# State-space hand-over by halves of the last down slice, low halves of y ahead of the second scan, later scans in parts

## The chip, the cores and the metric

The kernel runs on one core of one Trainium2 chip. The metric is the device time of one execution in microseconds (us). The core has a matrix engine (TensorE, PE in the profile; PEld is its weight load), a vector engine (VectorE, DVE), an activation engine (ScalarE, ACT), a general engine (GpSimd, POOL) and a queue of DMA issues (SyncE, SP). Each engine runs its own instructions in the order in which the program was laid out for it, and waits for others by semaphores.

## The reference

A trunk of two layers over 256 tokens with 2048 features, all in float32. Layer 0 mixes tokens with a convolution module, layer 1 with a state-space module; each is followed by a dense MLP.

```
x = x + conv_module(rms_norm(x))         # layer 0
x = x + mlp(rms_norm(x))                 # relu(h @ w_up)^2 @ w_down, 2048 -> 8192 -> 2048
# layer 1: h = rms_norm(x), 128 groups of 16 features, 64 complex states each
s_t = a * s_{t-1} + B u_t                # scan over the 256 tokens
y   = gelu(C s + d * h)
x   = x + val * sigmoid(gate)            # val, gate = split(y @ w_glu), 2048 -> 4096
x = x + mlp(rms_norm(x));  out = rms_norm(x)
```

## The kernel before

**Weights.** All dense weights stream through the core once. A *step* is one 1 MB tile of weights (`raw`), loaded by an SP DMA into one of three slots, and it has two *halves*. `split` (L109) makes of each half a rounded high part (`hi`, a copy on ACT, L117) and a remainder (`lo`, a subtraction on DVE, L119), each into one of four slots, and TensorE multiplies three times, hi by hi, lo by hi and hi by lo. `run_steps` (L148) walks the halves: before it consumes half h it issues splits up to half h + 3, so that the split of half h + 4 can start when half h has been consumed and its slot is free. Splits have a high priority in the list that the planner sorts by. The planner lays out each engine's order by a simulated timeline; `behind(ins)` (L391) makes the instructions of a block follow `ins` on its own engine.

**The last down slice of layer 0.** `mlp.down` (L697) multiplies by w_down in slices of 512 output columns. The last slice is consumed by `consume_by_block` (L712): it holds the weights of all its four halves, finishes token block 0 first, then the first 256 columns of block 1, then the other 256. After each piece `last_add` (L748) adds it to x and sums squares (on ACT for the first two pieces, on DVE for the last), and `block_rstd` (L760) makes the norm factor of a block; `ssm_block` (L166) turns the factors into the small matrix `rs` and starts the last `ssm_slice` (L1107), which writes a slice of x to DRAM and reads it back as `xJ`, tokens in chunks of eight.

**The state-space module.** Its input is cut into four parts B = 0 to 3 of 512 features. For one part: `chunks` (L1132) reorders xJ and turns it on PE (`ut`), `ssm_scale` multiplies by the norm factors, `ssm_front` (L1203) multiplies by the table W and copies to X, `ssm_turn` (L1219) turns X into PSUM (`xtr`), `ssm_scan` (L1230) does on DVE six products and sums, two scans, two products that turn back, and four sums into `SS`; `ssm_local` (L1263) multiplies by M, `ssm_carry` (L1278) by V onto the same banks, and takes the GELU on ACT into `y`; `ssm_out` (L1294) turns y (`yt`) and splits it into hi and lo as `yT`, with `hsplit` (L224).

**The GLU.** `glu` (L1308) has 16 steps, numbered (i, half). `begin` (L1321) stands between the last down step and the first GLU step and runs parts 0 and 1 of the state-space work: the first four GLU halves are split there (`more`, L1315), two before the first scan, one behind it, one behind the second. `keep_warm` (L173) puts multiplications by the identity on PE between the pieces. The first GLU product needs both halves hi and lo of yT of part 0. The rest of the state-space work is hung onto GLU steps by the dictionary `todo` (L1383): part 1 is multiplied at steps 1 and 2, parts 2 and 3 follow in pieces from step 1 to step 12. In it `chunk3` (L1358) turns part 3's input at step (3, 1), and `ssm_scan(2)` and `ssm_scan(3)` stand at (3, 0) and (6, 1), each as a whole.

Of the kernel before, what the change touches and what calls it, by code (L numbers as in the profile page):

```python
# [18 lines left out]
P = 128  # L19
# [17 lines left out]
class Trunk:  # L37
# [71 lines left out]
    def split(self, h, urgent=True):  # L109
        i, half = divmod(h, 2)  # L110
        raw = self.raws[i] if half == 0 else self.raws.pop(i)
        nk = raw.shape[1] // 2
        sl = raw[:, half * nk:(half + 1) * nk]
        hi = self.w.tile([P, nk] + list(raw.shape[2:]), F32R, tag="hi", name="hi", bufs=4)
        lo = self.w.tile([P, nk] + list(raw.shape[2:]), F32R, tag="lo", name="lo", bufs=4)
        with self.tc.high_priority(offset=URGENT if urgent else 0):
            self.nc.scalar.activation(hi, sl, AF.Copy)  # L117
            eng = self.nc.gpsimd if i in self.pool_lo else self.nc.vector
            ins = eng.tensor_tensor(out=lo, in0=sl, in1=hi.bitcast(F32), op=ALU.subtract)  # L119
            if i in self.pool_lo:  # L120
                self.pool_ins = ins
        self.parts[h] = (hi, lo)

# [24 lines left out]
    def run_steps(self):  # L148
        n = 2 * len(self.steps)
        ns = 0  # L150
        for h in range(n):
            i, half = divmod(h, 2)
            _, _, consume, pre = self.steps[i]
            if i == self.barrier and half == 0:
                self.barrier = None
                self.presplit = h
                pre()
                pre, ns = None, self.presplit
            while self.loaded < min(len(self.steps), i + 4):
# [12 lines left out]

    def keep_warm(self, n, after):  # L173

        ps = self.bank([P, P], name="warm")
# [496 lines left out]
    def mlp(self, layer, last_slice, last_block, hooks=None):  # L672
# [24 lines left out]
        def down(s):  # L697
            for n in range(NS):
                by_block = s == nsl - 1 and n == NS - 1
                for kc in range(2):  # L700
# [38 lines left out]
                    self.add_t(w_dn, s * 8 + kc * 4, n * 512, consume_by_block if by_block else consume,  # L739
# [367 lines left out]
    def ssm_slice(self, n):  # L1107
# [36 lines left out]
        def transposes(xr):  # L1144
            for g in range(0, 8, 4):
                ps = self.bank([P, 4, P], name="ut")
                for gg in range(4):
                    nc.tensor.transpose(ps[:, gg, :], xr[:, g + gg].rearrange("p t c -> p (t c)"), self.ident)
# [28 lines left out]
    def ssm_start(self):  # L1177
# [3 lines left out]
        with self.behind(self.mm_last):  # L1181
            self.late[0]()
        self.keep_warm(6, self.mm_last)
        nc.tensor.matmul(ps, lhsT=self.rowsel.rearrange("p t c -> p (t c)"),
                                   rhs=rs.rearrange("p b j -> p (b j)"), start=True, stop=True)
# [44 lines left out]
    def ssm_scan(self, B):  # L1230

        nc = self.nc
        ps, R = self.X.pop(B), self.tables.pop(("R", B))
# [16 lines left out]
        for i in range(2):  # L1250
            nc.vector.tensor_tensor_scan(out=flat(S[:, i]), data0=flat(m), data1=flat(S[:, i]), initial=0.0,
                                         op0=ALU.mult, op1=ALU.add)
        b = lambda i: R[:, i].unsqueeze(1).broadcast_to([P, 2, 16, 32])
        self.tt(t[:, 0], b(0), S, ALU.mult)
        self.tt(t[:, 1], b(1), S, ALU.mult)
# [22 lines left out]
    def ssm_carry(self, B):  # L1278
# [5 lines left out]
        if B == 0:  # L1284
            self.keep_warm(16, self.mmm)
        for g in range(8):
# [21 lines left out]
    def glu(self):  # L1308
# [6 lines left out]
        def more(n, xev=None):  # L1315
            for _ in range(n):
                with self.behind(self.scaled), self.behind(xev or self.scaled):
                    self.split(self.presplit, False)
                self.presplit += 1

        def begin():  # L1321
# [5 lines left out]
            more(2)  # L1327
# [23 lines left out]
            more(1, xev)  # L1351
# [5 lines left out]

        def chunk3():  # L1358
            late = []
            self.chunks[3](late)  # L1360
            with self.behind(self.mm_last):
                late[0]()
            self.ssm_scale(3)
# [15 lines left out]

        def front(B):  # L1380
            with self.behind(self.mm_last):
                self.ssm_front(B)
        todo = {(1, 0): (lambda: local(1), lambda: self.ssm_scale(2)), (1, 1): (lambda: carry(1),),  # L1383
                (2, 0): (lambda: out(1), lambda: front(2)), (2, 1): (lambda: turn(2),),
                (3, 0): (lambda: self.ssm_scan(2),), (3, 1): (chunk3,), (5, 0): (lambda: local(2),),
                (6, 0): (lambda: front(3),), (6, 1): (lambda: turn(3), lambda: self.ssm_scan(3)),
# [125 lines left out]
```

## Time and profile before

| | |
|---|---|
| device time, median of 3 runs (lowest to highest) | 2012.29 us (2011.23 to 2012.68) |
| the profiled execution: device time, span in the trace | 2011.6 us, 2009.8 us |
| PE busy, share of the span | 1977.3 us, 98% |
| PEld, DVE, ACT, POOL busy | 1693.9, 1399.2, 950.4, 280.6 us |
| mean granted TensorE clock | 0.996 |
| DMA | 428.49 MB, mean 213 GB/s |

Times in the rows below are counted from the first instruction of the span; the difference between device time and span, 1.8 us, lies around it. The last down slice of layer 0 runs from 1046 to 1057 us, `begin` from there to about 1088, the GLU steps to about 1294, and the MLP of layer 1 after that.

### The profile page before, as it was taken

How to read it: one execution, taken by the hardware profiler on the slowest of the kernel's cores; microseconds unless marked ns; L12 is line 12 of the kernel's file. 1: busy time of each engine (PE TensorE's matmuls, PEld its weight loads, DVE VectorE, ACT ScalarE, POOL GpSimd, SP SyncE). 2: the span in 40 equal slices, each digit the busy share in tenths (PEclk: the TensorE clock that was granted, in tenths of full speed). 3: DMA queues.
4: the chain of work that ended last, by engine and by line, in shares of the span. 5: the costliest groups of instructions: out<-in, count | busy, mean ns of one | idle time of the engine just before them, and what ended most of it. 6: DMA issues, size and time to landing. Idle time of an engine off the chain costs nothing.

```text
span 2009.8 us, 28976 instructions
## 1 busy us (share of the span) xinstructions
PE 1977.3 (98%) x11640; PEld 1693.9 (84%) x11640; DVE 1399.2 (70%) x1905; ACT 950.4 (47%) x1172; POOL 280.6 (14%) x257
## 2 busy tenths in 40 slices
PE   8999999999999999999998999999999999999998
PEld 8999787888888888888886788888888888888887
DVE  7899899967776777776557747565556555565655
ACT  6444654444444544444443445554444444444444
POOL 3998301000000221222010000000000000000000
PEclk9999999999999999999999999999999999999999
DMA  8668458766866877877887865665656666575653
GB/s 233 190 173 217 141 199 262 229 228 191 262 189 188 220 235 245 263 249 241 321 287 269 285 210 184 194 181 186 199 187 191 188 189 195 184 223 185 198 189 126
DMA packets 317030, 428.49 MB, mean 213 GB/s; under 512 B 9761, under 2 KB 211553, under 8 KB 313537
## 3 DMA queue, kind: packets, MB, share of 16 engines
q1 hardware_dynamic: 301120, 384.85, 60.9%
q0 software_dynamic: 12352, 37.49, 6.2%
q10 hardware_dynamic: 3424, 4.30, 0.8%
q8 instruction: 91, 1.49, 0.3%
q14 instruction: 43, 0.35, 0.0%
HBM read 400.08 MB, written 34.91 MB: 216 GB/s over the span
## 4 chain that ended last, share of the span: by engine, by line
PE 92%; DVE 5%; DMA 1%; issue 1%; POOL 0%; ACT 0%; ACTq 0%; SPq 0%; POOLq 0%; DVEq 0%
PE acc L187 23%; PE acc L210 15%; PE acc L212 15%; PE acc L211 15%; PE acc L190 12%; PE acc L199 3%; PE acc L201 3%; PE acc L200 3%; DVE lo L119 1%; DVE S L791 1%; PE pk L472 1%; DMA raw<-in_conv_w_in_dram 1%; DVE ws L791 1%; PE kp L1084 0%; DMA raw<-in_mlp_w_up_dram 0%
## 5 line engine op out<-in xcount | busy, mean ns | idle before, releaser
L117 ACT ACTIVATE hi<-raw 128x1024 fp32r<-128x1024 f32 x672 | 711.8, 1060 | 968.0 <-PE acc L212 524.8
L119 DVE TENSOR_TENSOR lo<-raw,hi 128x1024 fp32r<-128x1024 f32 x612 | 747.6, 1223 | 522.2 <-ACT hi L117 513.2
L187 PE MATMUL acc<-hT,hi 128*128 128x512 f32 x2048 | 516.1, 394 | 3.0 <-DVE t L779 2.1
L187 PEld LDWEIGHTS acc<-hT,hi 128*128 128x128 f32 x2048 | 369.7, 189 | 72.2 <-DVE t L779 2.4
L210 PE MATMUL acc<-hi,rT 128*128 128x512 f32 x992 | 387.4, 391 | 0.0
L211 PE MATMUL acc<-lo,rT 128*128 128x512 f32 x992 | 386.3, 389 | 0.0
L212 PE MATMUL acc<-hi,rT 128*128 128x512 f32 x992 | 385.9, 389 | 0.0
L190 PEld LDWEIGHTS acc<-hT,lo 128*128 128x128 f32 x2048 | 279.5, 190 | 20.9 <-DVE lo L119 0.8
L190 PE MATMUL acc<-hT,lo 128*128 128x256 f32 x2048 | 286.1, 282 | 0.4 <-DVE lo L119 0.4
L210 PEld LDWEIGHTS acc<-hi,rT 128*128 128x128 f32 x992 | 186.2, 188 | 39.9 <-issue 1.8
L212 PEld LDWEIGHTS acc<-hi,rT 128*128 128x128 f32 x992 | 186.2, 188 | 39.1
L211 PEld LDWEIGHTS acc<-lo,rT 128*128 128x128 f32 x992 | 186.3, 188 | 37.8
L119 POOL TENSOR_TENSOR lo<-raw,hi 128x1024 fp32r<-128x1024 f32 x60 | 143.3, 2406 | 31.3 <-ACT hi L117 31.2
L199 PE MATMUL acc<-hT,hi 128*128 128x256 f32 x512 | 146.2, 286 | 1.1 <-ACT hi L117 1.0
L200 PE MATMUL acc<-hT,hi 128*128 128x256 f32 x512 | 145.7, 286 | 0.0
L201 PE MATMUL acc<-hT,lo 128*128 128x256 f32 x512 | 145.5, 286 | 0.0
L800 DVE SCALAR_TENSOR_TENSOR cv<-vT,dw,cv 128x256 f32<-128x256 f32 x348 | 141.2, 482 | 2.2 <-ACT cv L515 1.7
L791 DVE TENSOR_TENSOR x<-x,acc 128x1024 f32<-128x1024 f32 (+1 forms) x72 | 83.6, 1161 | 33.5 <-PE acc L212 22.8
L212 PE MATMUL acc<-hi,yT 128*128 128x512 f32 x256 | 101.7, 397 | 4.8 <-DVE yT L226 4.8
L210 PE MATMUL acc<-hi,yT 128*128 128x512 f32 x256 | 102.6, 401 | 1.3 <-ACT hi L117 1.3
L211 PE MATMUL acc<-lo,yT 128*128 128x512 f32 x256 | 101.2, 395 | 1.6 <-DVE lo L119 1.6
L199 PEld LDWEIGHTS acc<-hT,hi 128*128 128x128 f32 x512 | 98.9, 193 | 3.4 <-ACT hi L117 1.7
(274 smaller groups left out, 1732.7 us busy)
## 6 DMA issues: line engine op xcount, KB each, us to landing
raw<-in_mlp_w_up_dram SPq DMA_DIRECT2D x128, 1024.0 KB, 5.8
raw<-in_mlp_w_down_dram SPq DMA_DIRECT2D x128, 1024.0 KB, 5.2
raw<-in_ssm_w_glu_dram SPq DMA_DIRECT2D x32, 1024.0 KB, 5.5
raw<-in_conv_w_in_dram SPq DMA_DIRECT2D x60, 512.0 KB, 5.6
raw<-in_conv_w_out_dram SPq DMA_DIRECT2D x16, 1024.0 KB, 5.2
Vd<-bv POOLq DMA_DIRECT2D x16, 512.0 KB, 4.9
Md<-Kd POOLq DMA_DIRECT2D x32, 256.0 KB, 7.9
Wt<-Wd SPq DMA_DIRECT2D x8, 1024.0 KB, 8.6
```

Source lines behind the costliest of these rows:

```text
L117: self.nc.scalar.activation(hi, sl, AF.Copy)
L119: ins = eng.tensor_tensor(out=lo, in0=sl, in1=hi.bitcast(F32), op=ALU.subtract)
L187: mm(accs[m], lhsT=hi[:, kk, cs[m]], rhs=xT(k0 + kk), start=first and kk == 0, stop=False)
L190: mm(accs[m][:, 0:T], lhsT=lo[:, kk, cs[m]], rhs=xT(k0 + kk)[:, 0, :], start=False, stop=last and kk == 3)
L199: mm(accs[m], lhsT=hi[:, kk, c], rhs=x[:, 0, :], start=first and kk == 0, stop=False)
L200: mm(accs[m], lhsT=hi[:, kk, c], rhs=x[:, 1, :], start=False, stop=False)
L201: mm(accs[m], lhsT=lo[:, kk, c], rhs=x[:, 0, :], start=False, stop=last and kk == 3)
L210: mm(acc[:, b, :], lhsT=ak[:, 0, t], rhs=hi[:, kk, :], start=first and kk == 0, stop=False)
L211: mm(acc[:, b, :], lhsT=ak[:, 0, t], rhs=lo[:, kk, :], start=False, stop=False)
L212: self.mm_last = mm(acc[:, b, :], lhsT=ak[:, 1, t], rhs=hi[:, kk, :], start=False, stop=last and kk == 1)
L791: self.nc.vector.tensor_tensor(out=out, in0=a, in1=b, op=op)
L800: return self.nc.vector.scalar_tensor_tensor(out=out, in0=a, scalar=s, in1=b, op0=op0, op1=op1)
```

## The change

Four things change. (1) In layer 0 the last down slice is consumed half by half (`consume_by_half`): each half is multiplied into all three pieces at once, and in the last half each piece is added to x as it is finished. Up to three GLU halves may then be split ahead of `begin` by the ordinary walk. (2) In `begin` the two splits ahead of the first scan and the one behind it are gone, one split remains behind the scans of part 1; part 3's reordering and turn (`chunks[3]`) come from step (3, 1) into `begin`, behind part 2's; the warming multiplications are 8 instead of 16 ahead of the first carry, and they follow part 3's turn; the carry takes the groups of the first SS half before those of the second. (3) `ssm_scan` is cut into three functions, and the scans of part 1 are put behind the low half of part 0's yT. (4) For parts 2 and 3 the scans, the products behind them and the sums into SS stand at steps of their own, each behind the newest low half of the weights (`lo_ins`).

```diff
@@ split, run_steps
             if i in self.pool_lo:
                 self.pool_ins = ins
+            else:
+                self.lo_ins = ins
...
-                self.presplit = h
+                self.presplit = ns
...
-            while ns < min(n, h + 4, n if self.barrier is None else 2 * self.barrier):
+            while ns < min(n, h + 4, n if self.barrier is None else 2 * self.barrier + 3):
@@ hsplit
-        self.nc.vector.tensor_tensor(out=lo, in0=raw, in1=hi.bitcast(F32), op=ALU.subtract)
+        self.low = self.nc.vector.tensor_tensor(out=lo, in0=raw, in1=hi.bitcast(F32), op=ALU.subtract)
@@ mlp.down
+                    def consume_by_half(hi, lo, half, kc=kc):
+                        if kc == 0 and half == 0:
+                            rT["acc"] = self.acc2()[:, 0, :], *(self.bank([P, 256], name="acc") for _ in range(2))
+                        h = kc * 2 + half
+                        for i, (b, c) in enumerate(((0, slice(0, 512)), (1, slice(0, 256)), (1, slice(256, 512)))):
+                            with self.behind(self.mm_last):
+                                self.mm_b(rT["acc"][i], lambda kk: rT[s][:, 2 * h + kk], hi, lo, b, c, h == 0, h == 3)
+                            if h == 3:
+                                self.last_add(b, int(i == 2), c, rT["acc"][i])
+                                if i:
+                                    last_block(i - 1)
...
+                               consume if not by_block else consume_by_block if layer else consume_by_half,
@@ ssm_start
-        with self.behind(self.mm_last):
+        self.keep_warm(6, self.mm_last)
+        with self.behind(self.mm_last), self.behind(self.sq):
             self.late[0]()
-        self.keep_warm(6, self.mm_last)
...
+        self.keep_warm(3, ins)
@@ ssm_scan: cut into ssm_scan (products, sums, scans), ssm_forth (two products), ssm_states (SS)
+        with self.behind(first) if first is not None else nullcontext():
+            for i in range(2):
+                ins = nc.vector.tensor_tensor_scan(out=flat(S[:, i]), data0=flat(m), data1=flat(S[:, i]), initial=0.0,
+                                                   op0=ALU.mult, op1=ALU.add)
+        return ins
+    def ssm_forth(self, B, ins):
...
+        with self.behind(ins):
+            self.tt(t[:, 0], b(0), S, ALU.mult)
+            self.tt(t[:, 1], b(1), S, ALU.mult)
@@ ssm_carry
-        if B == 0:
-            self.keep_warm(16, self.mmm)
-        for g in range(8):
+        for g in (0, 2, 4, 6, 1, 3, 5, 7):
@@ glu.begin
             self.ssm_turn(0)
-            more(2)
             self.ssm_scale(1)
...
                 self.chunks[2](late)
+                self.chunks[3](late)
             with self.behind(self.mmm):
                 late[0]()
+            with self.behind(self.ut):
+                late[1]()
+            ps = self.acc2("warm")[:, 0, 0:P]
+            self.keep_warm(8, self.ut, ps)
             get("W", 2)
-            self.ssm_scan(0)
+            self.ssm_forth(0, self.ssm_scan(0))
+            self.ssm_states(0)
             self.ssm_carry(0)
-            self.keep_warm(4, self.vmm)
-            more(1, xev)
+            self.keep_warm(4, self.vmm, ps)
             self.ssm_out(0)
-            self.keep_warm(5, self.yt)
-            self.ssm_scan(1)
-            more(1, xev)
+            self.keep_warm(3, self.yt, ps)
+            def more(ins):
+                with self.behind(ins), self.behind(xev):
+                    ins = self.split(self.presplit, False)
+                self.presplit += 1
+                return ins
+            self.ssm_forth(1, more(self.ssm_scan(1, self.low)))
+            self.ssm_states(1)
@@ glu: each of scan, forth, states of parts 2 and 3, and scale3, stands behind self.lo_ins
-                (3, 0): (lambda: self.ssm_scan(2),), (3, 1): (chunk3,), (5, 0): (lambda: local(2),),
-                (6, 0): (lambda: front(3),), (6, 1): (lambda: turn(3), lambda: self.ssm_scan(3)),
+                (3, 0): (lambda: scan(2),), (4, 0): (lambda: forth(2),), (4, 1): (lambda: states(2),),
+                (5, 0): (lambda: local(2), scale3), (6, 0): (lambda: front(3),),
+                (6, 1): (lambda: turn(3), lambda: scan(3)), (7, 1): (lambda: forth(3),), (8, 1): (lambda: states(3),),
```

## Rows read from the trace of the kernel before

**Rows 1.** Page, part 4: the chain that ended last, share by engine.

```profile
PE 92%; DVE 5%; DMA 1%; issue 1%; POOL 0%; ACT 0%; ACTq 0%; SPq 0%; POOLq 0%; DVEq 0%
```

**Rows 2.** Busy time by stretch: window, length, PE PEld DVE ACT POOL, clock, DMA, GB/s.

```profile
1066.00:1072.00 6.00, 5.38 (x116) 4.08 (x107) 5.96 (x9) 4.67 (x7) 0.41 (x1) 1.00 0.55 152
...
1082.00:1087.70 5.70, 0.89 (x6) 0.45 (x5) 5.70 (x7) 0.00 (x0) 0.00 (x0) 0.78 1.00 406
1087.70:1092.10 4.40, 4.38 (x10) 3.47 (x11) 4.31 (x6) 0.00 (x0) 0.00 (x0) 0.51 0.27 101
```

**Rows 3.** Timeline, PE: start, us, engine, line, operation, count, [idle before <-releaser].

```profile
1087.72 0.79 PE L212 MATMUL acc<-hi,yT 128*128 128x512 f32 x1 [4.83 <-DVE yT L226]
...
1092.11 0.39 PE L210 MATMUL acc<-hi,yT 128*128 128x512 f32 x1
...
1094.62 0.39 PE L212 MATMUL acc<-hi,yT 128*128 128x512 f32 x1
...
1124.86 1.04 PE L1148 MATMUL ut<-ident,xr 128*128 128x128 f32 x8
...
1127.15 0.50 PE L210 MATMUL acc<-hi,yT 128*128 128x512 f32 x1 [1.25 <-ACT hi L117]
...
1129.28 0.56 PE L211 MATMUL acc<-lo,yT 128*128 128x512 f32 x1 [1.63 <-DVE lo L119]
...
1133.27 0.39 PE L212 MATMUL acc<-hi,yT 128*128 128x512 f32 x1
```

**Rows 4.** Timeline, end of the last down slice and start of `begin`.

```profile
1053.26 0.69 DVE L791 TENSOR_TENSOR x<-x,acc 128x512 f32<-128x512 f32 x1 [4.31 <-PE acc L222]
...
1054.05 0.63 ACT L755 ACTIVATE junk<-x 128x512 f32<-128x512 f32 x1 [5.11 <-DVE x L791]
...
1057.14 1.99 ACT L117 ACTIVATE hi<-raw 128x1024 fp32r<-128x1024 f32 x2
...
1057.58 0.42 DVE L791 TENSOR_TENSOR x<-x,acc 128x256 f32<-128x256 f32 x1 [1.48 <-PE acc L222]
```

**Rows 5.** Timeline, up to the first scan of part 0.

```profile
1064.40 0.42 PEld L1226 LDWEIGHTS xtr<-ident,X 128*128 128x128 f32 x4 [0.36 <-ACT X L1216]
1064.49 1.22 DVE L119 TENSOR_TENSOR lo<-raw,hi 128x1024 fp32r<-128x1024 f32 x1
...
1065.63 2.41 DVE L791 TENSOR_TENSOR S<-R,xtr 128x496 f32<-128x496 f32 x4
```

**Rows 6.** Timeline, from the first scan to the first GLU products.

```profile
1065.90 2.51 SPq L91 DMA_DIRECT2D xJ<-xs  x4
...
1072.01 3.84 PE L178 MATMUL warm<-ident 128*128 128x128 f32 x32 [0.31 <-ACT xJ L1149]
...
1075.81 0.69 DVE L791 TENSOR_TENSOR SS<-S 64x512 f32<-64x512 f32 x1
...
1077.24 1.23 DVE L119 TENSOR_TENSOR lo<-raw,hi 128x1024 fp32r<-128x1024 f32 x1
1077.27 1.74 PE L1288 MATMUL acc<-Vt,SS 128*32 128x128 f32 x56 [1.01 <-DVE SS L1260]
...
1079.07 1.09 ACT L1292 ACTIVATE y<-acc 128x512 f32<-128x512 f32 x2 [6.63 <-PE acc L1288]
...
1080.90 1.08 ACT L225 ACTIVATE yT<-yt 128x512 fp32r<-128x512 f32 x2 [0.74 <-PE yt L1300]
...
1081.88 2.33 DVE L1251 TENSOR_TENSOR_SCAN S<-m,S 128x512 f32<-128x512 f32 x2
...
1084.13 0.67 DVE L226 TENSOR_TENSOR yT<-yt,yT 128x512 fp32r<-128x512 f32 x1
...
1086.98 0.68 DVE L226 TENSOR_TENSOR yT<-yt,yT 128x512 fp32r<-128x512 f32 x1
```

**Rows 7.** Timeline, ACT at the turn of part 3.

```profile
1125.56 0.60 ACT L1149 ACTIVATE xJ<-ut 128x512 f32<-128x512 f32 x1 [3.02 <-PE ut L1148]
```

**Rows 8.** DMA of tile xJ, 1030 to 1130 us, issue to landing.

```profile
DMA to landing us min/median/max: 2.7/3.8/8.5
```

More of the change, by code (lines that the diff above doesn't have):

```diff
@@ L171, in run_steps, with keep_warm @@
             self.tick()
-    def keep_warm(self, n, after):
-        ps = self.bank([P, P], name="warm")
+    def keep_warm(self, n, after, ps=None):
+        ps = self.bank([P, P], name="warm") if ps is None else ps
         with self.behind(after):
@@ L1147, in transposes @@
                 for gg in range(4):
-                    nc.tensor.transpose(ps[:, gg, :], xr[:, g + gg].rearrange("p t c -> p (t c)"), self.ident)
+                    self.ut = nc.tensor.transpose(ps[:, gg, :], xr[:, g + gg].rearrange("p t c -> p (t c)"), self.ident)
                 nc.scalar.activation(self.xJ[:, n, g:g + 4, :], ps, AF.Copy)
@@ L1180, in ssm_start @@
         ps = self.bank([P, 32], name="rj")
-        with self.behind(self.mm_last):
+        self.keep_warm(6, self.mm_last)
+        with self.behind(self.mm_last), self.behind(self.sq):
             self.late[0]()
-        self.keep_warm(6, self.mm_last)
-        nc.tensor.matmul(ps, lhsT=self.rowsel.rearrange("p t c -> p (t c)"),
+        ins = nc.tensor.matmul(ps, lhsT=self.rowsel.rearrange("p t c -> p (t c)"),
                                    rhs=rs.rearrange("p b j -> p (b j)"), start=True, stop=True)
@@ L1228, in ssm_turn, with ssm_scan @@
         self.X[B] = ps
-    def ssm_scan(self, B):
+    def ssm_scan(self, B, first=None):
         nc = self.nc
-        ps, R = self.X.pop(B), self.tables.pop(("R", B))
+        ps, R = self.X.pop(B), self.tables["R", B]
         S, t = self.S[:, 0], self.S[:, 2:4]
@@ L1249, in ssm_scan, with ssm_states @@
         flat = lambda x: x.rearrange("p g j -> p (g j)")
-        for i in range(2):
-            nc.vector.tensor_tensor_scan(out=flat(S[:, i]), data0=flat(m), data1=flat(S[:, i]), initial=0.0,
-                                         op0=ALU.mult, op1=ALU.add)
-        b = lambda i: R[:, i].unsqueeze(1).broadcast_to([P, 2, 16, 32])
-        self.tt(t[:, 0], b(0), S, ALU.mult)
-        self.tt(t[:, 1], b(1), S, ALU.mult)
+        with self.behind(first) if first is not None else nullcontext():
[4 more added lines that the diff above has]
+    def ssm_forth(self, B, ins):
+        nc = self.nc
+        R = self.tables.pop(("R", B))
+        S, t = self.S[:, 0], self.S[:, 2:4]
+        b = lambda i: R[:, i].unsqueeze(1).broadcast_to([P, 2, 16, 32])
+        with self.behind(ins):
+            self.tt(t[:, 0], b(0), S, ALU.mult)
+            self.tt(t[:, 1], b(1), S, ALU.mult)
+    def ssm_states(self, B):
+        nc = self.nc
+        t = self.S[:, 2:4]
         SS = self.t4([P, 16, 2, 32], name="SS")
@@ L1313, in glu @@
         get = self.table
[L1315 to L1319, printed above, removed]
         def begin():
@@ L1356, in turn @@
             return self.xtr
[L1358 to L1363, printed above, removed]
         def out(B):
@@ L1378, in carry, with scan, forth, states @@
             return self.vmm
+        def scan(B):
+            self.ssm_scan(B, self.lo_ins)
+        def forth(B):
+            self.ssm_forth(B, self.lo_ins)
+        def states(B):
+            with self.behind(self.lo_ins):
+                self.ssm_states(B)
         def front(B):
@@ L1382, in front, with scale3 @@
                 self.ssm_front(B)
+        def scale3():
+            with self.behind(self.lo_ins):
+                self.ssm_scale(3)
         todo = {(1, 0): (lambda: local(1), lambda: self.ssm_scale(2)), (1, 1): (lambda: carry(1),),
                 (2, 0): (lambda: out(1), lambda: front(2)), (2, 1): (lambda: turn(2),),
-                (3, 0): (lambda: self.ssm_scan(2),), (3, 1): (chunk3,), (5, 0): (lambda: local(2),),
-                (6, 0): (lambda: front(3),), (6, 1): (lambda: turn(3), lambda: self.ssm_scan(3)),
+                (3, 0): (lambda: scan(2),), (4, 0): (lambda: forth(2),), (4, 1): (lambda: states(2),),
+                (5, 0): (lambda: local(2), scale3), (6, 0): (lambda: front(3),),
+                (6, 1): (lambda: turn(3), lambda: scan(3)), (7, 1): (lambda: forth(3),), (8, 1): (lambda: states(3),),
                 (7, 0): (lambda: carry(2),), (8, 0): (lambda: out(2),), (9, 0): (lambda: local(3),),
```

3 lines of the change are left out of this document (2 added, 1 removed).

## The prediction, written before the changed kernel was run

> **What bounds the kernel now.** I read the page's chain first: TensorE carries 92% of it, VectorE (DVE) 5%, everything else about 1% or less [rows 1]. So a change outside TensorE's own work can only pay where TensorE stands still or runs slowly, and the next view is TensorE's timeline, searched for idle time. From the first GLU product on there are two places. The first is the hand-over: two GLU products are issued at 1082, then TensorE waits 4.83 us for the low half of yT and starts again at 1087.72 [rows 3]; its busy time in that stretch is 0.89 of 5.70 us, and in the next 4.4 us the granted clock is 0.51, which is the 1.2 GHz level [rows 2]. The second is at 1125.90: after eight turns (ut) TensorE waits 1.25 us for a high half and 1.63 us for a low half of weights, and again runs slowly behind it [rows 3]. Elsewhere from there to the last matmul it is full, so what is saved at these two places should reach the end of the kernel undiminished.
>
> In the hand-over DVE is the engine that ends last: from 1061 to 1087 it has no gap worth naming, and what it does is an order of work, not a quantity. The high halves of yT are finished at 1081.98 (1080.90 and 1.08, [rows 6]), but the first low half runs at 1084.13, behind two scans, and the second at 1086.98, behind two products of part 1 which nobody on TensorE is waiting for. Three low halves of GLU weights (1.15 to 1.2 us each) stand in the same DVE queue ahead of that, two before the first scan, one at 1077.24 [rows 5, 6].
>
> **The change part by part.**
>
> *Last down slice by halves.* The number of products is the same, so TensorE's end stays at 1057.4. What moves is their order. Before, block 0 was added to x at 1053.26, 4.3 us ahead of the last addition at 1057.58 [rows 4]. Now block 0 is finished only when the last half is: 12 products of 256 columns (12 x 0.12 us, estimated as half the 0.228 us that 512 take) ahead of the end, at about 1056.0. In return half a step's slot of hi and lo is free after every half, and three GLU splits go there. The last of them has its high half at about 1054.8 to 1055.8 on ACT and its low half at 1055.8 to 1057.0 on DVE, ahead of block 0's addition. Then the additions follow (0.69, 0.42, 0.42, [rows 4]) and end at 1058.4, not 1058.0; on ACT two squares (0.63 and, estimated by width, 0.4, with their read-outs) end near 1058.9, and block 1's norm factor needs both. I take +0.9 us for rs and all that follows; bounds +0.2 (the addition goes ahead of the low half, squares hidden) and +2.1 (one more 1.2 us low half in between).
>
> *Two low halves gone ahead of the first scan.* Together 2.3 us of DVE, but not 2.3 us of path. The scan's first product starts at 1065.63; without the low half at 1064.49 it would wait for the four turns that start at 1064.40, behind ACT's second copy of X, and last some 0.65 us [rows 5]. So it could start at 1065.1: 0.5 us gained, net of the step before 0.4 lost, 1066.0. SS is then complete at 1077.65 where it was 1077.2.
>
> *Carry.* Of its 64 products 56 run behind the last part of SS, in 1.74 us [rows 6]; with the groups of the first SS half ahead, 32 remain, 1.0 us, if TensorE is free when that half is ready (before: at 1075.8, now 1076.2). What stands ahead on TensorE now is part 3's turn: xJ of part 3 is issued from 1065.90 to 1068.4 and lands 3.8 us later [rows 6, 8], with the 0.5 us by which x itself is late at 1072.7; 1.05 us of reordering on ACT (as the copies of that size, [rows 4]), 1.0 us of turns [rows 3], 16 warming passes in 1.9 us (half of 32 in 3.84, [rows 6]): free at 1076.9. So carry ends at 1078.9, y starts on ACT at 1079.0 as before (1079.07), and hi of yT is ready at 1081.4 and 1081.9.
>
> *Low halves ahead of the second scan.* The third weight low half is gone from 1077.24, so the six products and sums of part 1 run from 1077.65 to 1081.15 (before 1078.4 to 1081.88). The two low halves follow as soon as hi is there: 1081.4 and 1082.05. Before, TensorE started 0.74 us after the second one did [rows 3, 6]; now at 1082.8. Gain against 1087.72: 4.9 us (bounds 3.9 and 5.6 from the +0.9 above).
>
> *Clock.* Without a 5 us hole I expect no fall of the clock. Ten spacings from 1087.72 take 4.39 us; eleven from 1092.11 to 1094.62 take 2.51, so ten take 2.28 [rows 3]. Gain 2.1 us.
>
> *Part 1 comes closer.* After the low halves DVE has two scans (2.3), the one remaining weight low half (1.2), products (2.2, the time between the two low halves of yT in rows 6), sums into SS (4 x 0.69), and two urgent weight low halves that become ready in between: from 1082.7 about 11 us, SS complete at about 1093.5. TensorE runs three halves (12 x 0.228 us each, two products of the first already issued) and the 64 products of `local` (2.0 us): carry of part 1 is due at 1092.5. Its first half finds SS ready at about 1092.1, its second at 1093.5, as the first ends. I take 0.5 us of wait (bounds 0 and 2). Before, this had several us of slack; it is what is late next.
>
> *Second place.* ACT had waited 3.02 us in its queue for part 3's turn, with weight splits queued behind it [rows 7]; TensorE then met a half whose split came late. With the turn in `begin` that queue does not form, and the DVE pieces (scans, products, sums) now stand behind low halves, not between. The 2.9 us of waiting should shrink to 0.4 (one pair of products, 2.2 us, may still push one low half); the slow clock there, ten spacings in 3.99 us instead of 2.28 [rows 3], gives back 1.7; the eight turns themselves, 0.9 us, move into a stretch where TensorE had only warming work. Gain 2.5 + 1.7 + 0.9 = 5.1 us. Bounds: 0.9 (both waits stay) and 5.5. DVE does no less than before; each low half has two halves' time, some 5 us, before TensorE needs it, and the largest backlog I count is 3 to 4 us.
>
> *Sum.* 4.9 + 2.1 + 5.1 - 0.5 = 11.6 us. The profiled execution took 2011.6 us (span 2009.8 and 1.8 around it): 2000.0. It lies 0.7 below the median of the runs, so for the median I forecast 2000.7 us.
>
> *A rule against it.* Between 1066 and 1072 TensorE did turns, small products and no dense work, and the granted clock stayed at 1.00 [rows 2]. The Trainium skill, "TensorE: Matmul & The Clock Gate", Part 4 (PE-mode transpose), says that transposes do not bring the full clock the way multiplications do; this change puts turns where 16 warming passes were. The trace speaks neither for nor against it, since there were warming passes close by; by that rule the third rival below would come true.
>
> **The rivals.**
>
> 1. *The second place stays.* TensorE met the late half there because its order was laid out so that it came early; if the order is laid out the same way and the pair of products on DVE holds it, both waits and the clock remain. For it: DVE still has the same pieces there. Against: the named releaser was ACT, behind the turn [rows 7]. Gain 11.6 - 4.2 = 7.4 us: 2004.9.
>
> 2. *Carry waits for part 3's turn.* TensorE's queue holds the turn and the warming ahead of carry, so each us by which xJ of part 3 comes later moves the restart by one, from a landing at about 1072 on. With the longest landing of that tile, 8.5 us [rows 8], the restart is at 1087.5: 4.7 us lost, 2.1 of clock lost, 2007.5. *The slower side:* the same mechanism, when ACT's order also puts that reordering ahead of part 2's and part 1's copies, so that the scans wait too. Every other gain (about 11.6 us) is eaten from a landing at 1084 on; at 1088 it gives 2016. For it: DMA is saturated at 1.00 while M, V and W load [rows 2]. Against: xJ is issued ahead of these loads.
>
> 3. *The clock falls in `begin`* for want of dense work. The last 32 carry products and the turns of y take twice their time (about 1.9 us more), and the first ten GLU products cost the 2.1 us again: 2004.7.
>
> 4. *It does not do what it says.* The low halves of yT stay late for another reason (hi itself late on ACT), and the later pieces wait as before: within 0.2% (4 us), 2011.
>
> **How the numbers follow.** My forecast 0.60; rival 1 0.13; rival 3 0.08; rival 2 0.05 in its milder form (faster still, by 4.8 us) and 0.08 in its slower one; rival 4 0.06. About 0.2%, 4 us, is what a measurement can tell from no change. Faster 0.60 + 0.13 + 0.08 + 0.05 = 0.86, same 0.06, slower 0.08. The forecast's own bounds add to a gain of 7.5 to 13.2 us if no rival comes true, mostly 9 to 13. For 8 in 10 I take 1996.5 at the low end (a little beyond all favourable bounds, since the planner may close a gap that I have not counted) and 2008.0 at the high end, which takes in rivals 1 and 3 and the milder 2.
>
> **What would show it.** In the trace of the changed kernel: the last wait on yT's low half under 1.5 us and TensorE back between 1082 and 1084; clock 1.00 from there on; the two low halves of yT next to each other on DVE, ahead of the scans; rs later by about 0.9 us than now; carry of part 1 with under 1 us of idle; no wait of ACT for ut past the first GLU product; no TensorE gap over 0.5 us between 1090 and 1140. Wrong would be: a TensorE gap behind part 3's turn with the carry waiting, a clock near 0.5 at the first products, a new gap of 2 us or more at the carry of part 1 or at a weight half behind one of the moved scans.

## The result, and the profile after

The changed kernel took 2001.09 us in the median of four runs (2000.04 to 2002.30), the kernel before 2012.49 us (2011.23 to 2013.07). The ratio is 0.9947, with an interval from 0.9932 to 0.9962: 0.5% faster. The forecast was 2000.7 us. The profiled execution after took 2002.3 us (span 2000.5), the slowest of its four; the one before 2011.6 (span 2009.8). So the two traces differ by 9.3 us, the medians by 11.4. Three executions among those of the experiments below (one each of the kernel before, of the turn alone and of the last slice by blocks) took 2792 to 8918 us and are left out of the ratios and ranges.

The chain of after by engine; DVE's 5% of [rows 1] is 3%, DMA and SP's queue have 1% more each:

```profile
PE 92%; DVE 3%; DMA 2%; issue 1%; SPq 1%; POOL 0%; ACT 0%; ACTq 0%; POOLq 0%; DVEq 0%
```

The windows of after, with the columns of [rows 2]. Against [rows 2], the last two of the hand-over (1082 to 1092.1) are full and at clock 1.00, as forecast, and so is the stretch of the second place but for half a microsecond. New is a granted clock of 0.70 at 1072 to 1077, ahead of them, a mean between the two levels of 1.2 and 2.4 GHz: 1.00 until 1074, then 0.50 to 0.52 until 1077.

```profile
1072.00:1077.00 5.00, 2.82 (x15) 2.71 (x14) 4.79 (x6) 3.23 (x5) 1.46 (x2) 0.70 0.91 367
...
1082.00:1087.70 5.70, 5.53 (x30) 4.34 (x29) 4.62 (x6) 1.74 (x3) 0.00 (x0) 1.00 0.99 411
1087.70:1092.10 4.40, 4.40 (x75) 3.50 (x75) 4.39 (x6) 1.47 (x2) 0.00 (x0) 1.00 1.04 385
1120.00:1130.00 10.00, 9.48 (x96) 7.74 (x97) 7.39 (x10) 2.88 (x3) 0.00 (x0) 1.00 0.63 214
```

TensorE's timeline of after (columns as in [rows 3]; the first GLU lines are now L213 to L215, and M's and V's products of a part, `acc` or `mv`, are L1305 and L1316):

```profile
1057.56 1.50 PE L181 MATMUL warm<-ident 128*128 128x128 f32 x12
...
1060.96 0.41 PE L1200 MATMUL rj<-rs,rowsel 128*128 128x32 f32 x2 [1.02 <-DVE rs L811]
...
1074.30 1.97 PE L1164 MATMUL ut<-ident,xr 128*128 128x128 f32 x8 [2.18 <-ACT xJ L1165]
1076.06 2.61 PE L181 MATMUL warm<-ident 128*128 128x128 f32 x16
1078.60 1.95 PE L1316 MATMUL acc<-Vt,SS 128*32 128x128 f32 x64
...
1084.42 0.50 PE L215 MATMUL acc<-hi,yT 128*128 128x512 f32 x1
...
1086.85 0.39 PE L213 MATMUL acc<-hi,yT 128*128 128x512 f32 x1
...
1094.48 1.95 PE L1316 MATMUL mv<-Vt,SS 128*32 128x128 f32 x64
...
1120.52 0.50 PE L214 MATMUL acc<-lo,yT 128*128 128x512 f32 x1 [0.63 <-DVE lo L119]
...
1123.24 1.98 PE L1305 MATMUL mv<-Mt,xJ 128*32 128x128 f32 x64
...
1163.98 0.63 PE L1316 MATMUL mv<-Vt,SS 128*32 128x128 f32 x8
1165.02 1.94 PE L1316 MATMUL mv<-Vt,SS 128*32 128x128 f32 x56 [0.41 <-DMA Vt<-Vd]
```

Beside the same instructions in the trace of before, these give the whole account. Each step is what is gained (-) or lost (+) from one point to the next:

| point | before | after | step |
|---|---|---|---|
| third GLU product starts | 1087.72 [rows 3] | 1084.42 | -3.30 |
| ten products later | 1092.11 [rows 3] | 1086.85 | -1.96 (clock) |
| M's products of part 2 | 1133.59 | 1123.24 | -5.09 (second place) |
| V's products of part 3, until the next GLU product | 1174.28 to 1176.19 | 1163.98 to 1166.89 | +1.00 (wait for V) |
| span | 2009.8 | 2000.5 | -9.30 in all |

The third step is 10.35 less the 5.26 of the first two. V's products of part 1, the carry that I expected to wait, stand at 1099.77 before and 1094.48 after, -5.29: no wait there. In the fourth row the same 64 products take 1.91 us before and 2.91 after, with the wait in between. The four steps add to -9.35.

```profile
1057.38 1.04 PE L1148 MATMUL ut<-ident,xr 128*128 128x128 f32 x8
...
1094.94 1.96 PE L1275 MATMUL mv<-Mt,xJ 128*32 128x128 f32 x64
...
1099.77 1.95 PE L1288 MATMUL mv<-Vt,SS 128*32 128x128 f32 x64
...
1133.59 1.98 PE L1275 MATMUL mv<-Mt,xJ 128*32 128x128 f32 x64
...
1174.28 1.98 PE L1288 MATMUL mv<-Vt,SS 128*32 128x128 f32 x64
```

These are TensorE's rows of before that the account needs beyond [rows 3]; the first one follows the last down slice (1057.38, in after 1057.56).

**Three places in after.** ACT's timeline shows why the carry came late in this execution: part 3's reordering (xr) stands ahead of part 2's copies out of PSUM (xJ<-ut) and waits 2.31 us for its DMA, and the turn of part 3 on TensorE is released by those copies (the line at 1074.30 above):

```profile
1072.70 1.06 ACT L1154 ACTIVATE xr<-xJ 128x1024 f32<-128x1024 f32 x1 [2.31 <-DMA xJ<-xs]
1073.66 1.07 ACT L1165 ACTIVATE xJ<-ut 128x512 f32<-128x512 f32 x2
```

DVE's timeline shows the new order: yT's low halves together, ahead of part 1's scan; in part 2 one or two low halves between scan, products and sums; then part 3's sums, four from 1150.62, ahead of the low half at 1153.43:

```profile
1083.08 1.29 DVE L229 TENSOR_TENSOR yT<-yt,yT 128x512 fp32r<-128x512 f32 x2 [2.10 <-ACT yT L228]
1084.29 2.33 DVE L1269 TENSOR_TENSOR_SCAN S<-m,S 128x512 f32<-128x512 f32 x2
1086.54 1.20 DVE L119 TENSOR_TENSOR lo<-raw,hi 128x1024 fp32r<-128x1024 f32 x1
...
1089.92 1.22 DVE L119 TENSOR_TENSOR lo<-raw,hi 128x1024 fp32r<-128x1024 f32 x1
...
1093.16 0.69 DVE L1290 TENSOR_TENSOR SS<-S 64x512 f32<-64x512 f32 x1
...
1112.49 2.33 DVE L1269 TENSOR_TENSOR_SCAN S<-m,S 128x512 f32<-128x512 f32 x2
1114.74 2.33 DVE L119 TENSOR_TENSOR lo<-raw,hi 128x1024 fp32r<-128x1024 f32 x2
1116.99 2.35 DVE L807 TENSOR_TENSOR S<-S 128x1024 f32<-128x1024 f32 x2
1119.26 1.21 DVE L119 TENSOR_TENSOR lo<-raw,hi 128x1024 fp32r<-128x1024 f32 x1
...
1150.62 0.68 DVE L807 TENSOR_TENSOR SS<-S 64x512 f32<-64x512 f32 x1
...
1153.43 1.23 DVE L119 TENSOR_TENSOR lo<-raw,hi 128x1024 fp32r<-128x1024 f32 x1
```

SP's queue shows whom that low half holds up. A weight load waits for its slot until 1154.69, and part 3's V is queued behind it. V's landing took up to 9.3 us, and TensorE was there at 1163.98:

```profile
1154.69 0.37 SPq L91 DMA_DIRECT2D raw<-in_ssm_w_glu_dram  x1
1155.15 0.93 SPq L91 DMA_DIRECT2D Vt<-Vd  x2
```

Before, V was issued at 1164.21 for a use at 1174.28. The load has moved by 9.06 us and its use by 10.30. Of the 1.24 us of difference 1.00 is lost on TensorE, so the load had next to no slack before.

### The profile page after: what moved, and what is told of

The parts are those of the page before. It is cut to its first block, busy times and chain, and to the rows that moved or that the text cites. A ratio compares the mean times of both kernels' runs of the same rounds, so it can differ in the third digit from the quotient of the medians.

```text
span 2000.5 us, 28951 instructions
## 1 busy us (share of the span) xinstructions
PE 1973.6 (99%) x11626; PEld 1691.4 (85%) x11626; DVE 1400.7 (70%) x1905; ACT 951.4 (48%) x1172; POOL 280.7 (14%) x257
## 4 chain that ended last, share of the span: by engine, by line
PE 92%; DVE 3%; DMA 2%; issue 1%; SPq 1%; POOL 0%; ACT 0%; ACTq 0%; POOLq 0%; DVEq 0%
PE acc L190 23%; PE acc L213 15%; PE acc L215 15%; PE acc L214 15%; PE acc L193 12%; PE acc L203 3%; PE acc L202 3%; PE acc L204 3%; DVE lo L119 1%; PE pk L475 1%; DMA raw<-in_conv_w_in_dram 1%; SPq L91 1%; DMA Vt<-Vd 0%; PE kp L1100 0%; DMA xs<-x 0%
## 5 line engine op out<-in xcount | busy, mean ns | idle before, releaser
L190 PEld LDWEIGHTS acc<-hT,hi 128*128 128x128 f32 x2048 | 368.8, 189 | 71.8 <-DVE t L795 2.4
L213 PE MATMUL acc<-hi,rT 128*128 128x512 f32 x992 | 387.4, 391 | 0.0
L215 PE MATMUL acc<-hi,rT 128*128 128x512 f32 x992 | 385.9, 389 | 0.0
L213 PEld LDWEIGHTS acc<-hi,rT 128*128 128x128 f32 x992 | 186.2, 188 | 39.7 <-issue 1.8
L215 PEld LDWEIGHTS acc<-hi,rT 128*128 128x128 f32 x992 | 186.2, 188 | 39.1
L202 PEld LDWEIGHTS acc<-hT,hi 128*128 128x128 f32 x512 | 98.7, 193 | 3.6 <-ACT hi L117 1.9
L213 PE MATMUL acc<-hi,yT 128*128 128x512 f32 x256 | 101.2, 395 | 0.1
L203 PEld LDWEIGHTS acc<-hT,hi 128*128 128x128 f32 x512 | 98.5, 193 | 2.2 <-issue 1.6
```

The lines of the kernel that those rows point to most:

```text
L190: mm(accs[m], lhsT=hi[:, kk, cs[m]], rhs=xT(k0 + kk), start=first and kk == 0, stop=False)
L202: mm(accs[m], lhsT=hi[:, kk, c], rhs=x[:, 0, :], start=first and kk == 0, stop=False)
L203: mm(accs[m], lhsT=hi[:, kk, c], rhs=x[:, 1, :], start=False, stop=False)
L213: mm(acc[:, b, :], lhsT=ak[:, 0, t], rhs=hi[:, kk, :], start=first and kk == 0, stop=False)
L215: self.mm_last = mm(acc[:, b, :], lhsT=ak[:, 1, t], rhs=hi[:, kk, :], start=False, stop=last and kk == 1)
```

## The experiments

Theory: the hand-over gains because yT's low halves pass ahead of the scan; the second place empties because scan, products and sums stand between low halves. Rivals: the second place empties because part 3's turn has left it (half of what the prediction said), or the slice by halves carries part of the gain. Not taken back one by one are the order of the groups in the carry, the number of warming passes, and the place of part 3's scaling, which goes along with the parts below.

**Low halves of yT first, nothing else** (before, with one edit: both of part 1's scans are placed behind yT's last low half):

```diff
-        self.nc.vector.tensor_tensor(out=lo, in0=raw, in1=hi.bitcast(F32), op=ALU.subtract)
+        self.low = self.nc.vector.tensor_tensor(out=lo, in0=raw, in1=hi.bitcast(F32), op=ALU.subtract)
...
-            self.ssm_scan(1)
+            self.ssm_scan(1, self.low)
```

> The kernel before with one edit: the two scans of part 1 stand behind the low half of part 0's yT. Theory (the order on VectorE is what held the first GLU products): the two low halves run side by side at about 1082 to 1083.3, TensorE is back at about 1083.8 instead of 1087.7, the clock stays at 1.00, and nothing else changes, so a gain of 3.9 + 2.1 = 6 us: 2006.3 us; the waits at part 3's turn (about 1.25 and 1.6 us) stay. Rival (the wait only moves: part 1's carry then waits for SS): TensorE waits 2 us or more at the carry of part 1 and the gain is under 3 us: above 2009.

Measured: 2005.18 us (2004.38 to 2006.39), ratio 0.9969 [0.9957, 0.9981]. TensorE's timeline:

```profile
1082.80 0.50 PE L212 MATMUL acc<-hi,yT 128*128 128x512 f32 x1 [0.33 <-DVE yT L226]
...
1120.23 0.50 PE L210 MATMUL acc<-hi,yT 128*128 128x512 f32 x1 [1.25 <-ACT hi L117]
...
1122.36 0.79 PE L211 MATMUL acc<-lo,yT 128*128 128x512 f32 x1 [1.63 <-DVE lo L119]
```

The hole of 4.83 us is 0.33, and both waits of the second place stay, to the hundredth as in [rows 3]. This one dependency takes 6.6 us off (2011.83 on this chip before), over half of the whole gain, and the second place does not change by it. The rival did not come: the carry of part 1 starts 6.92 us earlier than before, as M's products ahead of it do (1092.85 and 1088.02).

**Part 3's turn into `begin`, nothing else** (before, with one edit):

```diff
                 self.chunks[2](late)
+                self.chunks[3](late)
...
+            with self.behind(self.ut):
+                late[1]()
...
-                (3, 0): (lambda: self.ssm_scan(2),), (3, 1): (chunk3,), (5, 0): (lambda: local(2),),
+                (3, 0): (lambda: self.ssm_scan(2),), (3, 1): (lambda: self.ssm_scale(3),), (5, 0): (lambda: local(2),),
```

> The kernel before with one edit: part 3's input is reordered and turned in the stretch before the first GLU step, behind part 2's, and only its scaling stays at step (3, 1); the planner then also puts both low halves of yT behind part 1's two products. Theory (the turn at step (3, 1) made the second place): the two waits near 1127 and the slow clock behind them go, 5 us, while the turn and 32 warming passes behind it hold the first carry back by about 1.5 us: 2008.5 us. Rival (the second place comes from part 2's scans standing whole between the weight halves): the waits stay and the time is 2012 to 2014 us.

Measured: 2009.85 to 2014.17 us, ratio 1.0002 [0.9993, 1.0012], where 2008.5 was expected; the rival came true. The trace is that of the fastest execution. TensorE's timeline:

```profile
1074.44 1.14 PE L1148 MATMUL ut<-ident,xr 128*128 128x128 f32 x8 [2.92 <-ACT xJ L1149]
...
1127.49 0.50 PE L211 MATMUL acc<-lo,yT 128*128 128x512 f32 x1 [4.08 <-DVE lo L119]
```

The ACT queue of [rows 7] is gone, and the second place waits longer than before, 4.08 us, for a low half on DVE. So ACT's turn was not the cause there. At the hand-over this trace gains 2.3 us, 0.5 of it an earlier end of the slice: the wait for yT's low half is 1.97 us, the clock stays up, and M's products of part 1 start at 1092.63 (1094.94 before). The time shows no gain, because the second place costs more.

**Scans of parts 2 and 3 whole again** (after, with one edit; `whole` issues scan, products and sums of a part one after another, behind no given low half):

```diff
-                (3, 0): (lambda: scan(2),), (4, 0): (lambda: forth(2),), (4, 1): (lambda: states(2),),
-                (5, 0): (lambda: local(2), scale3), (6, 0): (lambda: front(3),),
-                (6, 1): (lambda: turn(3), lambda: scan(3)), (7, 1): (lambda: forth(3),), (8, 1): (lambda: states(3),),
+                (3, 0): (lambda: whole(2),), (3, 1): (lambda: self.ssm_scale(3),), (5, 0): (lambda: local(2),),
+                (6, 0): (lambda: front(3),), (6, 1): (lambda: turn(3), lambda: whole(3)),
```

> The changed kernel with the scans, products and sums of parts 2 and 3 whole again at steps (3, 0) and (6, 1) and part 3's scaling at (3, 1). Theory (moving the turn is what emptied the second place, the parts matter little): within 1 us of the changed kernel, 2001, with V of part 3 arriving a little earlier, so perhaps 2000. Rival (the parts are what emptied it): a wait of 2 us or more near 1120 and a slow clock behind it, 2004 to 2006.

Measured: 2005.25 us (2003.96 to 2007.63), ratio 0.9970 [0.9959, 0.9981], some 4 us more than after; the rival came true. The trace is that of the slowest execution. DVE's timeline, then TensorE's, then a window (columns as in [rows 2]):

```profile
1119.15 0.68 DVE L807 TENSOR_TENSOR SS<-S 64x512 f32<-64x512 f32 x1
...
1121.94 1.29 DVE L1217 TENSOR_TENSOR xJ<-xJ,rJ 128x512 f32<-128x512 f32 x2
1123.15 2.35 DVE L119 TENSOR_TENSOR lo<-raw,hi 128x1024 fp32r<-128x1024 f32 x2
```

```profile
1124.43 0.79 PE L214 MATMUL acc<-lo,yT 128*128 128x512 f32 x1 [4.08 <-DVE lo L119]
```

```profile
1120.00:1130.00 10.00, 5.92 (x35) 4.12 (x33) 5.46 (x7) 1.13 (x2) 0.00 (x0) 0.66 0.65 204
```

With the turn still in `begin`, the sums and the scaling run in one block and the low half behind them comes 4.08 us late; the granted clock is 0.66 over 1120 to 1130, and products follow each other by 0.42 us (1125.02, 1125.44), not 0.23. It is the same wait as with the turn alone. So what empties the second place is that low halves come between the pieces; the edit also puts the scaling (1.29 us) back ahead of the low half, and how much of the wait is the scaling's alone was not tried.

**The turn back in its old place** (after, with part 3's reordering and turn at (3, 1) as before, in a new `chunk3` without the scaling, which stays at (5, 0); the rest is kept):

```diff
-                self.chunks[3](late)
-            with self.behind(self.ut):
-                late[1]()
...
-                (3, 0): (lambda: scan(2),), (4, 0): (lambda: forth(2),), (4, 1): (lambda: states(2),),
+                (3, 0): (lambda: scan(2),), (3, 1): (chunk3,), (4, 0): (lambda: forth(2),), (4, 1): (lambda: states(2),),
```

> The changed kernel with part 3's reordering and turn back at step (3, 1); the parts of the scans stay where the change put them. Theory (the parts behind the low halves emptied the second place, and the turn in front of the first carry only costs): the first carry is not held, TensorE is back at about 1082.6 instead of 1084.4, the turn costs 0.9 us of TensorE between dense products, no wait over 1 us near 1125: 2000 us, 0 to 1.5 below the changed kernel's 2001. Rival (the turn is needed too, because weight splits queue behind it on ScalarE): a wait of 2 us or more near 1125 with a slow clock behind it, 2003 to 2005.

Measured: 2001.28 us (2000.65 to 2002.79), ratio 0.9953 [0.9941, 0.9966]: as after. The second place lies at 1110 to 1122 here:

```profile
1110.00:1120.00 10.00, 9.85 (x45) 7.87 (x44) 9.83 (x10) 6.33 (x8) 0.00 (x0) 1.00 0.89 317
```

TensorE is busy for 9.85 of 10 us at clock 1.00, so the second place stays empty without the moved turn: the rival is refuted. The eight turns are back among the GLU products (1.04 us), and the time does not show it. At the hand-over TensorE is back at 1082.31, as expected; the 2 us against the first execution of after are not in the median, and the second execution of after, below, is back as early with the turn in `begin`.

**Last slice by blocks** (after, with one edit; the three low halves stand in `begin`, two ahead of the first scan and one ahead of part 1's, as before):

```diff
-            while ns < min(n, h + 4, n if self.barrier is None else 2 * self.barrier + 3):
+            while ns < min(n, h + 4, n if self.barrier is None else 2 * self.barrier):
...
-                               consume if not by_block else consume_by_block if layer else consume_by_half,
+                               consume if not by_block else consume_by_block,
...
+            for _ in range(2):
+                with self.behind(self.scaled):
+                    self.split(self.presplit, False)
+                self.presplit += 1
...
```

> The changed kernel with the last down slice of layer 0 by blocks again, and with it two weight splits ahead of the first scan and one behind it. Theory from the trace of the changed kernel (part 3's turn on TensorE holds the first carry, so VectorE has over 2 us of slack ahead of the low halves): no difference beyond 0.5 us, 2001. Rival, as predicted (VectorE's chain ends last): the low halves come 0.5 to 1.2 us later and the time is 2001.6 to 2002.3.

Measured: 2001.51 us (2001.36 to 2001.97), ratio 0.9950 [0.9936, 0.9963]: as after. TensorE's timeline:

```profile
1060.11 0.41 PE L1200 MATMUL rj<-rs,rowsel 128*128 128x32 f32 x2 [0.19 <-DVE rs L811]
...
1083.42 0.50 PE L215 MATMUL acc<-hi,yT 128*128 128x512 f32 x1 [1.10 <-DVE yT L229]
```

rs is 0.85 us earlier than in after, and yT's low half is waited for 1.10 us: what the halves take at the start they give back at the end. Counted from the end of the slice (1057.55), TensorE is back after 25.87 us, in the changed kernel after 26.86 in its first execution and after 24.81 in its second (below). So where the clock stays up the halves are ahead by 1.1 us in the trace; the time does not show it, with an interval of 2.7 us to either side.

**The same kernel once more, and two ways at its leftovers.** After unchanged; after with its eight warming passes moved between part 2's turn and part 3's; with V of part 3 loaded one weight tile earlier; with both. In the first cut `kw` is the last warming product.

> The changed kernel once more, beside the two below on one chip. Theory (part 3's input lands just when TensorE has run out of work, so that in some executions the clock falls ahead of the first carry and in others not): times spread over 2 us or more, 2000 to 2002, and a profile shows either the idle time with a clock under 1.00 between 1072 and 1077, or neither. Rival (the spread seen so far is that of the measurement): a spread under 1 us.

```diff
-            with self.behind(self.ut):
-                late[1]()
             ps = self.acc2("warm")[:, 0, 0:P]
             self.keep_warm(8, self.ut, ps)
+            with self.behind(self.kw):
+                late[1]()
```

> The changed kernel with its 8 warming multiplications put between part 2's turn and part 3's turn, instead of behind both. Theory (in the changed kernel TensorE idles 2.2 us for part 3's input, the clock falls to half there, and turn and warming then take 4.3 us in front of the carry): the warming fills the idle time, the clock stays at 1.00, the carry starts at about 1076 instead of 1078.6, TensorE is back at about 1082.4, 2 us earlier: 1999.1 us. Rival (VectorE's chain or the arrival of part 3's input sets the end anyway): less than 0.7 us, 2000.4 to 2001.1.

```diff
-                                                                (11, (("M", 3),)), (14, (("V", 3),)))}
+                                                                (11, (("M", 3),)), (13, (("V", 3),)))}
```

> The changed kernel with the load of table V of part 3 issued one weight tile earlier. Theory (the moved sums of part 3 delay a weight low half, that delays a weight load, and V's load stands behind it in the DMA queue, so that part 3's carry waits): V lands before it is needed, the wait of about 1 us at the carry of part 3 goes: 2000.1 us. Rival (V's slot or the bandwidth holds it): the wait stays and the time is 2001.

> Both edits together: warming between the turns and V of part 3 one tile earlier. Theory: the two gains add, 2 + 1 us: 1998 us. Rival (one of the places only shifts its wait to the next, as the carry of part 1, which had no slack left): 1999.5 to 2001.

| kernel | us, median (range) | ratio |
|---|---|---|
| after, again | 2000.29 (1999.78 to 2004.81) | 0.9950 [0.9937, 0.9962] |
| warming | 2000.46 (2000.18 to 2001.16) | 0.9948 [0.9936, 0.9961] |
| V earlier | 1999.32 (1998.86 to 2001.05) | 0.9944 [0.9931, 0.9958] |
| both | 1999.03 (1998.44 to 1999.34) | 0.9940 [0.9928, 0.9953] |

The first row was taken on another chip than the other three; each ratio is to the kernel before on the same chip (2011.12 and 2010.60 us).

After, again (the window ahead of the carry, then TensorE's timeline):

```profile
1072.00:1077.00 5.00, 4.01 (x61) 3.62 (x65) 4.76 (x7) 2.51 (x5) 0.90 (x2) 1.00 1.02 428
```

```profile
1057.01 1.50 PE L181 MATMUL warm<-ident 128*128 128x128 f32 x12
...
1072.99 1.15 PE L1164 MATMUL ut<-ident,xr 128*128 128x128 f32 x8 [1.43 <-ACT xJ L1165]
1073.97 1.95 PE L181 MATMUL warm<-ident 128*128 128x128 f32 x16
1075.85 2.09 PE L1316 MATMUL acc<-Vt,SS 128*32 128x128 f32 x64
...
1087.04 1.95 PE L1305 MATMUL mv<-Mt,xJ 128*32 128x128 f32 x64
...
1162.52 1.94 PE L1316 MATMUL mv<-Vt,SS 128*32 128x128 f32 x56 [0.53 <-DMA Vt<-Vd]
```

The clock did not fall in this execution, and the carry, counted from the end of the slice, is 2.2 us earlier than in the first (18.84 us behind 1057.01, against 21.04 behind 1057.56). So the low clock is a matter of the single execution. Expected were idle time with a low clock, or neither; here TensorE is idle for 1.43 us and the clock stays at 1.00. The spread of over 2 us came (5.0). The fall goes with a later tile: counted from the end of the slice, the four issues of part 3's tile on SP's queue began at 9.24 and took 3.53 us in the first execution, and began at 8.51 and took 2.51 in this one. Two more kernels have the same `begin`. With the scans whole again ACT got the tile 15.28 us behind the end of the slice and the clock of 1072 to 1077 is 0.82; with V earlier it is 14.39 us and 1.00. The two executions of after have 15.14 us with 0.70 and 14.38 with 1.00.

V's wait is in both executions. With the earlier load it is gone, as expected, and all 64 products run in one stretch:

```profile
1161.59 1.96 PE L1316 MATMUL mv<-Vt,SS 128*32 128x128 f32 x64
```

With the warming moved in both, the earlier load is worth 1.4 us (1999.03 against 2000.46, on the same chip, ranges apart).

The moved warming was expected at 1999.1 us and missed; its rival came true. It fills the idle time (0.20 us is left ahead of part 3's turn, clock 1.00 over 1072 to 1077), but the carry then waits for DVE, 0.74 us and, in the middle, 0.36:

```profile
1075.89 1.08 PE L1316 MATMUL acc<-Vt,SS 128*32 128x128 f32 x32 [0.74 <-DVE SS L1290]
```

It changes V's version by 0.3 us, inside the ranges; both together are 1 us short of the 1998 expected. Its own runs spread over 1.0 us, those of after over 2.3 and 5.0, which may be the rarer low clock, but is not shown.

**Products and sums of part 2 together, on top of both edits** and, beside it on the same chip, both edits alone:

```diff
-                (3, 0): (lambda: scan(2),), (4, 0): (lambda: forth(2),), (4, 1): (lambda: states(2),),
+                (3, 0): (lambda: scan(2),), (4, 1): (lambda: forth(2), lambda: states(2)),
```

> Both edits as before, and the two products of part 2 one half later, at step (4, 1), so that the low half which TensorE waits for near 1120 comes ahead of them. Theory: the wait of 0.6 us there goes, 1998.4 us against 1999.0 without it. Rival (the next low half is then late instead): no difference.

> Warming between the turns and V of part 3 one tile earlier, once more, beside the changed kernel on one chip. Theory: 2 us below the changed kernel, with a spread under 1 us. Rival: within 0.7 us of it.

Measured: 1997.91 us (1997.85 to 1999.81), ratio 0.9936 [0.9922, 0.9949], beside 1998.70 (1998.21 to 1999.12), ratio 0.9937 [0.9925, 0.9950]. In its trace the last 0.63 us of the second place are gone; in that of both edits alone they are there. The step of 0.8 us is inside the ranges. In the medians the version as a whole is 13.2 us below the kernel before (2011.12 there) and 2.4 us below the changed one. Both edits alone are 1.6 us below the changed one, where 2 were expected and under 0.7 by the rival.

## Why the prediction was right, and where it was not

**Hand-over: forecast 4.9, measured 3.3.** The place and the cause are right: the dependency alone brings TensorE back at 1082.80 (its slice ended 0.4 us earlier than before), the time that I gave for the whole change. In the changed kernel's profiled execution it came at 1084.42. DVE was on time (products and sums of part 1 done at 1080.98, forecast 1081.15) and then waited 2.10 us for the high half. The step that failed is "free at 1076.9": the landing that I put at 1072.7 was right (1072.70), but on ACT part 3's reordering then runs ahead of part 2's two copies out of PSUM, and the turn is released by those. It started at 1074.30, 0.5 us behind the reordering's end (1073.76). The clock was at its lower level through the turn and into the warming: 4.30 us from 1074.30 to 1078.60 where I had 2.9. Carry ended 1.6 us late, and yT with it. With the turn back in its old place the carry starts at 1075.92 and TensorE is back at 1082.31, so it is the turn that held it. No run puts the copies ahead of the reordering. In the second execution ACT's order is the same, but the tile came earlier and the clock stayed up: there M's products of part 1 start 7.9 us earlier than before (1087.04), of which 0.4 is an earlier end of the slice: 7.5 where hand-over and clock together were forecast at 7.0.

**Clock behind the hand-over: forecast 2.1, measured 1.96.** Right.

**Rivals 2 and 3** came true in part, in two of the four profiled executions with this `begin`: carry did wait for part 3's turn, and the clock fell ahead of it (0.70 and 0.82 over 1072 to 1077). Of the prediction's own signs, TensorE back between 1082 and 1084 was missed by 0.4 us in the profiled execution. The Trainium skill, "TensorE: Matmul & The Clock Gate", Part 4 (PE-mode transpose), says that the full clock does not engage for transposes, which do not count as busy in the same way. The runs do not settle whether that happened here. All four did the same turns; TensorE stood still for 2.18 and 2.06 us ahead of part 3's in the two whose clock fell, for 1.43 and 1.09 us in the two whose clock did not. With the turn alone moved it stood still for 2.92 us, did the same turns, and the window from 1072 to 1077 shows clock 1.00, in one execution; what decides stays open:

```profile
1072.00:1077.00 5.00, 2.30 (x18) 1.99 (x19) 4.76 (x7) 3.12 (x5) 0.86 (x2) 1.00 0.99 329
```

**Slice by halves and low halves ahead of the first scan.** The cost was as forecast (TensorE's product with rs starts 1.02 us later, 0.18 of it the slice's end; I had 0.9); its return, three low halves fewer on DVE in `begin`, is in the trace and not in the time.

**Carry of part 1: forecast -0.5, measured 0.** From the end of yT's low halves (1084.37) to complete sums DVE took 9.5 us, not 11: two weight low halves came in between (1086.54, 1089.92), I had counted three.

**Second place: forecast 5.1, measured 5.1, for the wrong reason.** The three terms (waiting from 2.88 to 0.63, the clock, the turn gone) hold. But the step "with the turn in `begin` that queue does not form" is false as a cause: it does not form, and the wait is still there, 4.08 us, on DVE. I had read the releaser of one wait, ACT behind the turn, and not asked who would be late next: the sums and the scaling on DVE. The other half of the same sentence, the pieces behind low halves, carries waiting and clock: without it some 4 us are lost (2005.25), where those two terms were 2.5 and 1.7, and it holds without the moved turn (2001.28).

**Not in the prediction: V of part 3, +1.00.** A load's issue is tied to a slot that DVE frees; a use that moves up by more than its load does eats the slack. It is "what is late next" on a queue that I had not followed: SP's.

So the sum of 11.6 stands on terms that were 7.0, 5.1 and -0.5, and measured, in the execution without the low clock, 7.5, 5.1, 0 and about -1.1. What I missed and what I overcharged nearly cancel, so it is in part luck that the total came this close.

Three sums in the prediction are off without touching the forecast. Its terms for "free at 1076.9" (1072.7, 1.05, 1.0, 1.9) add to 1076.65. The low bound of the hand-over, from +2.1 us in place of +0.9, is 3.7 and not 3.9. The low bounds as stated (3.9, 2.1, 0.9, -2) add to a gain of 4.9 and not 7.5.

## What to carry to other kernels

A trace names the last of several releasers of a wait; before taking its removal as the gain, take it out of the queue in thought and read which engine would release the same wait then. Where an engine serves urgent and patient work from one queue, cutting the patient work into pieces behind given urgent ones paid more than moving work elsewhere, and one dependency brought over half of it. When a stage moves up, check every load whose issue hangs on something that does not move with it.

## What the runs showed of the hardware that I had not expected

In the window with 2.18 us of idle time ahead of part 3's turn TensorE's clock was 0.70, and in the kernel with the turn alone moved, with 2.92 us in the same place, 1.00: the length of that one idle time did not decide it here. Among the four executions with the same `begin` the two whose tile came late (15.14 and 15.28 us behind the slice) had the clock fall, the two whose tile came early (14.38 and 14.39) not. The same four DMA issues on SP's queue took 2.51 or 2.52 us in ten of thirteen profiled executions and 3.49 to 3.71 us in three; why is open.
